# Float32r products that read their streamed operand from two halves in turn

## The chip, the cores and the metric

The kernel runs on one core of one Trainium2 chip. The metric is the device time of one execution in microseconds; lower is better. Times named before and after are medians of several executions.

## The reference

One transformer layer over 256 tokens of width 2048, in float32: a gated feed-forward, a token mixer with eight attention heads and four mLSTM heads, and a second gated feed-forward. Each is preceded by a modulation and followed by a layer norm. Almost all of the work lies in the weight matrices.

```
def _swiglu(h, w_in, w_out):                       # w_in 2048 x 11264, w_out 5632 x 2048
    gate, up = jnp.split(h @ w_in, 2, axis=-1)
    return (jax.nn.silu(gate) * up) @ w_out

def _token_mixer(h, w_in, ..., w_out):             # w_in 2048 x 6160, w_out 2048 x 2048
    z = h @ w_in
    ...                                            # attention of 8 heads, mLSTM of 4 heads
    return jnp.concatenate([y_fox, y_mlstm], axis=-1) @ w_out

def _layer(x, c, ...):
    ada = (silu(c) @ w_ada + b_ada)[:, None, :]    # w_ada 2048 x 18432
    sh1, sc1, g1, sh2, sc2, g2, sh3, sc3, g3 = jnp.split(ada, 9, axis=-1)
    h = _swiglu(_modulate(x, sh1, sc1), ffn1_w_in, ffn1_w_out)
    x = _layernorm(ALPHA * x + 0.5 * (1 + g1) * h, ln1_g, ln1_b)
    h = _token_mixer(_modulate(x, sh2, sc2), w_in, ..., w_out)
    x = _layernorm(ALPHA * x + (1 + g2) * h, ln2_g, ln2_b)
    h = _swiglu(_modulate(x, sh3, sc3), ffn2_w_in, ffn2_w_out)
    return _layernorm(ALPHA * x + 0.5 * (1 + g3) * h, ln3_g, ln3_b)
```

## The kernel before

**Split products.** A float32 operand is cut into two float32r parts: hi, a rounded copy made by ScalarE (line 155), and lo, the difference made by VectorE (line 156). A product of two float32 tiles is then the sum of three float32r products, hi by hi, hi by lo and lo by hi, added up in one PSUM tile. This is mm3 (lines 406 to 409), which all large products go through. In the profile the three show as lines 407, 408 and 409. A matmul takes a stationary operand, 128 columns that are loaded as weights before it (PEld in the profile), and a streamed one, whose words go through the array.

**Two forms.** Where features come out on partitions (the input products of the feed-forwards, tiles s, gu_f, fh, fs; the heads' inputs, tiles pr), the weight matrix is stationary and the 256 tokens are streamed, xhi or xlo, 256 columns. Where tokens come out on partitions (the output products o_f and o_mx, the mixer's tiles mo, b_mv, b_fv, and ge, gf), the tokens are stationary and 512 columns of weights are streamed; two blocks in b_mv and b_fv are 256 and 264 columns wide, since 8 gate columns follow the values there. Some early products of mo and ge take whole float32 operands (line 734), which need no split.

**Order.** The first feed-forward's input runs in four parts as the modulated features become ready (first_in, to about 308 us), then in column blocks (ffn_in, tiles gu_f, to 528 us); then its output products with three widths of columns (out_proj, to 774 us), a boundary with the layer norm, the mixer (to 1163 us), another boundary, the second feed-forward's input (tiles ge, fh, gf, fs, gu_f, to 1667 us) and its output (to 1910 us), and the last layer norm. Beside all this the weights of the modulation, w_ada, are loaded and summed on VectorE (line 170) a few rows at a time, put between the steps.

**Weights.** SyncE issues one load of 1 MB per step (line 382) into one of three raw buffers; hi and lo have six buffers each. Small gaps between tiles (gap) fix where in SBUF the tiles lie.

**PSUM.** Five tiles of 128 x 512 float32 take the large products, three more the small ones. A finished tile is read by ScalarE or VectorE: the gated product in ffn_in (lines 432, 433), the residual update in out_proj (lines 486, 488, 497, 499), copies elsewhere. In the two staged inputs (first_in, and fh with fs) the parts are kept in hT in the order in which PSUM held them, and the gated product comes later (lines 949 and 950; 1593 to 1597).

Of the kernel before, what the change touches and what calls it, by code (L numbers as in the profile page):

```python
# [14 lines left out]
P = 128  # L15
# [17 lines left out]
def layer_kernel(  # L33
# [344 lines left out]
    def load_w(src, nk, w, name, by_parts=False, behind=None, into=None):  # L378
# [5 lines left out]
        for q in range(nk // h):  # L384
# [18 lines left out]
            for kk in range(h):  # L403
                yield q * h + kk, hi[:, kk, :], lo[:, kk, :]

    def mm3(o, ah, al, bh, bl, start, stop):
        PE.matmul(o, ah, bh, start=start, stop=False)  # L407
        PE.matmul(o, ah, bl, start=False, stop=False)  # L408
        PE.matmul(o, al, bh, start=False, stop=stop)  # L409


    def cols_form_a(src, c0, outs, xT, name, npump, halves=(0, 1)):
        xhi, xlo = xT
        for kh in halves:
            for k8, hi, lo in load_w(src[kh * 1024:(kh + 1) * 1024, c0:c0 + 256], 8, 256, f"{name}_{kh}"):
                k = kh * 8 + k8
                for f in range(2):
                    fs = slice(f * P, (f + 1) * P)
                    mm3(outs[f], hi[:, fs], lo[:, fs], xhi[:, k, :], xlo[:, k, :],
                        k == 8 * halves[0], k == 8 * halves[-1] + 7)  # L420
            npump()

    def ffn_in(w, xT, hT, j0, tag, npump):
        for j in range(j0, DFF // 256):
            ps = [mm_tile(f"gu_{tag}{j}_{f}") for f in range(2)]
            for gu in range(2):
                last = gu and j == DFF // 256 - 1
                cols_form_a(w, gu * DFF + j * 256, [p[:, gu * T:(gu + 1) * T] for p in ps], xT,
                            f"{tag}i{j}_{gu}", (lambda: None) if last else npump)
            for f in range(2):  # L430
                sg = sm.tile([P, T], F32, tag="sg", bufs=2, name=f"sg_{tag}{j}_{f}")
                S.activation(sg, ps[f][:, :T], AF.Silu)
                pin["h"] = V.tensor_tensor(out=hT[:, 2 * j + f, :], in0=sg, in1=ps[f][:, T:], op=ALU.mult).ins
        for _ in range(2):
            npump()

# [2 lines left out]
    def out_proj(w, rows, nk, tag, npump, finish, before=None, turned=False, spare=None, fine=None):  # L439
# [12 lines left out]
        for width in (1024, 512, 512):  # L452
# [29 lines left out]
            def add_halves(outs, col=col):  # L482
                for c, o in enumerate(outs):
                    cs = slice(col + c * 256, col + (c + 1) * 256)
                    r = res[:, 1, cs]
                    V.tensor_tensor(out=o[:, :256], in0=o[:, :256], in1=gate[:, cs], op=ALU.mult)
                    yield
                    V.tensor_tensor(out=r, in0=r, in1=o[:, :256], op=ALU.add)
                    yield
                    add_stats(cs)  # L490
                    yield

            def add_up(a, ps=ps, col=col, bs=range(nb), stats=True):
                for b in bs:
                    cs = slice(col + b * 512, col + (b + 1) * 512)
                    r = res[:, a, cs]
                    V.tensor_tensor(out=ps[a, b], in0=ps[a, b], in1=gate[:, cs], op=ALU.mult)
                    yield
                    V.scalar_tensor_tensor(out=r, in0=r, scalar=ALPHA, in1=ps[a, b],
                                           op0=ALU.mult, op1=ALU.add)  # L500
                    yield
                    if a and stats:
                        add_stats(cs)
                    elif stats:
                        V.bn_stats(st[0][:, col // 512 + b, :], r)
                    yield
# [216 lines left out]
    def cols_1024(raws, xs, ws, split_, load, ps, xT, npump, u0, u1, ready=None):  # L723
        def split_products(a, k, hi, lo, start, stop):
            ts_ = slice(a * P, (a + 1) * P)
            for b in range(2):
                bs = slice(b * 512, (b + 1) * 512)
                mm3(ps[a, b], xT[0][:, k, ts_], xT[1][:, k, ts_], hi[:, bs], lo[:, bs], start, stop)

        for a, u in ((0, 0), (0, 1), (0, 2), (1, 2)) if raws else ():  # L730
            for q in range(2):
                k = 2 * u + q
                for b in range(2):
                    PE.matmul(ps[a, b], xs[a, k], raws[u][:, q, b * 512:(b + 1) * 512], start=k == 4 * a, stop=False)
        for w in ws:
            split_products(1, *w, False, False)
        for u in range(u0 + len(raws), u1):
            if u == u1 - 2 and ready:
                ready()
            for w in split_.get(u) or load(u):  # L740
                for a in range(2):
                    split_products(a, *w, w[0] == 2 * u0, w[0] == 2 * u1 - 1)
            npump()
# [178 lines left out]
    def first_in(j, i, ws):  # L922
        gu, q = i % 2, i // 2
        pss = [mm_tile(f"s{j}_{i}_{b}") for b in range(2)]
        def one(h, k, hi, lo, start, stop):
            for b, ps in enumerate(pss):
                fs = slice((2 * b + h) * P, (2 * b + h + 1) * P)
                mm3(ps[:, h * T:(h + 1) * T], hi[:, fs], lo[:, fs], xT[0][:, k, :], xT[1][:, k, :], start, stop)

        ws = list(ws)  # L930
        if i + j == 0:
            for w in ws:
                for h in range(2):
                    one(h, *w, w[0] + h == 0, w[0] + h == 4)
        else:
            for h in range(2):
                for w in ws:
                    one(h, *w, w[0] == 4 * j, w[0] == 4 * j + 3)
        for b, ps in enumerate(pss):
            f0 = 2 * NS * gu + 4 * q + 2 * b  # L940
            part = first_part(f0, f0 + 2).rearrange("p f t -> p (f t)")
            if j == 0:
                copied[i] = S.copy(part, ps).ins
            else:
                pin["h"] = V.tensor_tensor(out=part, in0=part, in1=ps, op=ALU.add).ins
            if j == 3 and gu:
                for f in range(f0, f0 + 2):
                    sg = sm.tile([P, T], F32, tag="sg", bufs=2, name=f"sgs{f}")
                    S.activation(sg, hT[:, f - 2 * NS, :], AF.Silu)
                    V.tensor_tensor(out=hT[:, f - 2 * NS, :], in0=sg, in1=first_part(f, f + 1)[:, 0, :], op=ALU.mult)  # L950

    ws = []

# [225 lines left out]

    def use_fv(col, a, ps, w):  # L1180
        wv = min(w, 1024 - col)
        out_ = S.copy(yF[:, col // P:(col + wv) // P, a * P:(a + 1) * P],
                      ps[:, :wv].rearrange("p (h n) -> p h n", n=P))
        if wv < w:
            out_ = S.copy(gz[:, a, 0:8], ps[:, wv:w])
            V.tensor_tensor(out=gz[:, a, 0:8], in0=gz[:, a, 0:8], in1=gbias[:, 0:8], op=ALU.add)
        return out_
# [73 lines left out]
    def use_mv(col, a, ps, w):  # L1261
        wv = min(w, 1024 - col)
        for i in range(0, wv, MV):
            out_ = S.copy(yM[(col + i) // MV][:, a, :MV], ps[:, i:i + MV])
        if wv < w:
            S.copy(gz[:, a, 12:16], ps[:, wv:wv + 4])
            out_ = S.copy(gz[:, a, 8:12], ps[:, wv + 4:w])
            V.tensor_tensor(out=gz[:, a, 8:12], in0=gz[:, a, 8:12], in1=gbias[:, 12:16], op=ALU.add)
            V.tensor_tensor(out=gz[:, a, 12:16], in0=gz[:, a, 12:16], in1=gbias[:, 8:12], op=ALU.add)
        return out_  # L1270
# [143 lines left out]

    for a in range(2):
        for h in range(NMH):
            emptied[0] = S.activation(og[h][:, a, :MV], mps[a, h // 2][:, h % 2 * MV:(h % 2 + 1) * MV],
                                      AF.Sigmoid).ins
    cols_form_b(C_FV, 512, [256, 264], use_fv, "fv")
    cols_form_b(C_MV, 512, [256, 264], use_mv, "mv")  # L1420
# [8 lines left out]
    def fox_heads(h0, name, before):  # L1429
        qs = {}  # L1430

        def queries():
            for h in range(h0, h0 + 4):
                qs[h] = new_qk(f"qs{h}", before(h))
                S.mul(qs[h][:, 0, :], psq[h - h0], QK_SCALE)

        psq = form_a_four(C_FQ + h0 * P, f"f{name}")
        psk = form_a_four(C_FK + h0 * P, f"f{name}k", queries)
        for h in range(h0, h0 + 4):
            S.copy(qs[h][:, 1, :], psk[h - h0])  # L1440
            side.append(fox_head(qs[h], h))

    for i, c0 in enumerate((C_MQ, C_MK)):
# [4 lines left out]
        for u in us:  # L1448
            V.memset(u[:, :, 0:4], 0.0)
        for h in range(NMH):  # L1450
            S.copy(us[h // 2][:, h % 2, 4:], ps[h])
        if i == 0:
            os_ = [new_qk(f"o_{h}", ()) for h in range(NMH)]
        side.append(conv_part(us, os_, i))
# [89 lines left out]

    for a in range(2):
        for g in range(2):
            S.copy(part(a, g), gups[a, g])

    def half_in(j, kh, tag):
        ps = [mm_tile(f"{tag}{j}_{f}") for f in range(2)]  # L1550
# [25 lines left out]
    cols_1024([], {}, [], {}, gu_load, gups, xT, at(R_B), 4, 8, lambda: [None for _ in mb])  # L1576
    for a in range(2):
        for g in range(2):
            V.tensor_tensor(out=part(a, g), in0=part(a, g), in1=gups[a, g], op=ALU.add)
        S.activation(part(a, 0), part(a, 0), AF.Silu)  # L1580
        V.tensor_tensor(out=part(a, 0), in0=part(a, 0), in1=part(a, 1), op=ALU.mult)
    for j in range(2, 10):
# [7 lines left out]
        for f in range(2):  # L1590
# [3 lines left out]
            V.tensor_tensor(out=u, in0=u, in1=ps[f][:, T:], op=ALU.add)  # L1594
            sg = sm.tile([P, T], F32, tag="sg", bufs=2, name=f"sgf{i}")
            S.activation(sg, g, AF.Silu)
            V.tensor_tensor(out=g, in0=sg, in1=u, op=ALU.mult)
    npool.release()
    ffn_in(W2, xT, hT, 10, "f2", at(R_B))
    need(14)  # L1600
# [44 lines left out]
```

## Time and profile before

| | |
|---|---|
| median of 3 runs | 1921.97 us (1921.58 to 1922.64) |
| span of the profiled execution | 1920.7 us |
| its chain that ended last: TensorE, VectorE, DMA | 91%, 4%, 3% |
| HBM read over the span | 506.71 MB, 265 GB/s |

No time of its own is listed for the profiled execution beside its span; the span stands 1.3 us below the median. A group row of the profile reads: line, engine, operation, written tile <- read tiles, shape, count | busy us, mean ns of one | idle time of the engine before them and who ended it. Records of successive matmuls overlap, so their mean is longer than the time between their starts. A row of the chain reads: start, duration, what. A row of the windows reads: window in us, its length, then for each engine its busy time and number of instructions, the granted clock of TensorE, the share of the DMA engines and GB/s.

### The profile page before, as it was taken

What the parts mean: (1) busy time and instruction counts of PE and PEld (TensorE: products, weight loads), DVE (VectorE), ACT (ScalarE), POOL (GpSimd) and SP (SyncE); (2) the same over time, 40 slices, a digit from 0 to 9 for tenths busy, and PEclk for the clock granted to TensorE, in tenths of its full rate; (3) what the DMA queues carried; (4) which work ended last, traced back from release to release, by engine and by line L of the source; (5) the groups of instructions that cost most, each with busy time, mean ns of one, the idle gap of its engine ahead of it and who ended that gap; (6) DMA issues with size and microseconds to landing.
All of it is one profiled execution on the core that took longest, in us unless ns stands there. A gap on an engine that the chain in (4) does not pass through costs nothing.

```text
span 1920.7 us, 32475 instructions
## 1 busy us (share of the span) xinstructions
PE 1892.3 (99%) x13161; PEld 1730.3 (90%) x13161; DVE 1482.5 (77%) x1855; ACT 948.7 (49%) x1358; POOL 60.0 (3%) x88
## 2 busy tenths in 40 slices
PE   7999999999999999999999999999999999999997
PEld 5999999999988887699999886999999999988886
DVE  6788988877788898878889888867766665555776
ACT  3554454443454555845565545555444444444562
POOL 1111100000000000100000000000000000000000
PEclk9999999999999999999999999999999999999999
DMA  9978968999898786499878983987777765655552
GB/s 365 379 279 310 314 235 273 331 311 329 282 343 304 263 308 222 147 312 323 306 270 308 310 306 130 336 293 241 257 251 260 248 212 188 241 188 187 195 196 89
DMA packets 283710, 510.92 MB, mean 266 GB/s; under 512 B 10626, under 2 KB 134178, under 8 KB 282536
## 3 DMA queue, kind: packets, MB, share of 16 engines
q1 hardware_dynamic: 276024, 482.10, 73.3%
q0 software_dynamic: 7536, 26.75, 4.2%
q8 instruction: 103, 1.69, 0.4%
q14 instruction: 47, 0.39, 0.1%
HBM read 506.71 MB, written 2.10 MB: 265 GB/s over the span
## 4 chain that ended last, share of the span: by engine, by line
PE 91%; DVE 4%; DMA 3%; ACT 1%; issue 1%; POOL 0%; SPq 0%; DVEq 0%; ACTq 0%; POOLq 0%
PE gu_f L409 8%; PE gu_f L407 8%; PE gu_f L408 8%; PE o_f L407 8%; PE o_f L409 7%; PE o_f L408 7%; PE s L409 4%; PE s L407 4%; PE s L408 4%; PE fh L407 2%; PE fh L409 2%; PE fh L408 2%; PE fs L407 1%; PE fs L408 1%; PE fs L409 1%; PE o_mx L407 1%
## 5 line engine op out<-in xcount | busy, mean ns | idle before, releaser
L170 DVE SCALAR_TENSOR_TENSOR acc<-ar,csil,acc 128x1024 f32<-128x1024 f32 (+1 forms) x167 | 211.6, 1268 | 67.2 <-DMA ar<-in_w_ada_dram 66.5
L409 PE MATMUL s<-xhi_f,lo_s 128*128 128x256 f32 x768 | 212.3, 277 | 0.7 <-DVE lo_s L156 0.6
L407 PE MATMUL s<-xhi_f,hi_s 128*128 128x256 f32 x768 | 212.6, 277 | 0.3 <-ACT xhi_f L336 0.3
L408 PE MATMUL s<-xlo_f,hi_s 128*128 128x256 f32 x768 | 212.4, 277 | 0.0
L409 PE MATMUL gu_f<-xhi_f,lo_f2i 128*128 128x256 f32 x768 | 212.0, 276 | 0.0
L407 PE MATMUL gu_f<-xhi_f,hi_f2i 128*128 128x256 f32 x768 | 212.0, 276 | 0.0
L408 PE MATMUL gu_f<-xlo_f,hi_f2i 128*128 128x256 f32 x768 | 212.0, 276 | 0.0
L156 DVE TENSOR_TENSOR lo_f2i<-raw_f2i,hi_f2i 128x1024 fp32r<-128x1024 f32 x96 | 117.6, 1225 | 94.1 <-ACT hi_f2i L155 94.1
L409 PE MATMUL gu_f<-xhi_f,lo_f1i 128*128 128x256 f32 x640 | 176.8, 276 | 0.1
L407 PE MATMUL gu_f<-xhi_f,hi_f1i 128*128 128x256 f32 x640 | 176.7, 276 | 0.0
L408 PE MATMUL gu_f<-xlo_f,hi_f1i 128*128 128x256 f32 x640 | 176.7, 276 | 0.0
L155 ACT CAST hi_f2i<-raw_f2i 128x1024 fp32r<-128x1024 f32 x96 | 100.8, 1050 | 135.4 <-PE gu_f L408 122.9
L155 ACT CAST hi_s<-raw_s 128x1024 fp32r<-128x1024 f32 x96 | 99.5, 1051 | 129.3 <-PE s L408 84.4
L409 PEld LDWEIGHTS s<-xhi_f,lo_s 128*128 128x128 f32 x768 | 144.1, 188 | 1.1 <-DVE lo_s L156 1.1
L408 PEld LDWEIGHTS s<-xlo_f,hi_s 128*128 128x128 f32 x768 | 144.2, 188 | 0.3 <-DVE xlo_f L339 0.3
L407 PEld LDWEIGHTS s<-xhi_f,hi_s 128*128 128x128 f32 x768 | 144.0, 188 | 0.4 <-ACT xhi_f L336 0.4
L407 PEld LDWEIGHTS gu_f<-xhi_f,hi_f2i 128*128 128x128 f32 x768 | 144.2, 188 | 0.2
L408 PEld LDWEIGHTS gu_f<-xlo_f,hi_f2i 128*128 128x128 f32 x768 | 144.2, 188 | 0.2
L409 PEld LDWEIGHTS gu_f<-xhi_f,lo_f2i 128*128 128x128 f32 x768 | 144.2, 188 | 0.0
L170 DVE SCALAR_TENSOR_TENSOR gate<-ar,csil,gate 128x1024 f32<-128x1024 f32 (+1 forms) x94 | 117.5, 1251 | 29.8 <-DMA ar<-in_w_ada_dram 29.4
L156 DVE TENSOR_TENSOR lo_f2o<-raw_f2o,hi_f2o 128x1024 fp32r<-128x1024 f32 x86 | 105.2, 1223 | 43.3 <-ACT hi_f2o L155 43.3
L156 DVE TENSOR_TENSOR lo_s<-raw_s,hi_s 128x1024 fp32r<-128x1024 f32 x96 | 115.3, 1220 | 25.5 <-ACT hi_s L155 25.4
(484 smaller groups left out, 5522.9 us busy)
## 6 DMA issues: line engine op xcount, KB each, us to landing
ar<-in_w_ada_dram SPq DMA_DIRECT2D x230, 512.0 KB, 5.3
raw_f2i<-in_ffn_w_in_dram SPq DMA_DIRECT2D x48, 1024.0 KB, 5.1
raw_s<-in_ffn_w_in_dram SPq DMA_DIRECT2D x47, 1024.0 KB, 7.5
raw_f1o<-in_ffn_w_out_dram SPq DMA_DIRECT2D x44, 1024.0 KB, 7.5
raw_f2o<-in_ffn_w_out_dram SPq DMA_DIRECT2D x44, 1024.0 KB, 5.1
raw_f1i<-in_ffn_w_in_dram SPq DMA_DIRECT2D x40, 1024.0 KB, 7.8
ar<-in_w_ada_dram POOLq DMA_DIRECT2D x45, 512.0 KB, 6.6
raw_mxo<-in_w_out_dram SPq DMA_DIRECT2D x16, 1024.0 KB, 7.6
```

What stands on the lines that cost most here:

```text
L155: S.copy(hi, src)
L156: return V.tensor_tensor(out=lo, in0=src, in1=hi.bitcast(F32), op=ALU.subtract)
L170: V.scalar_tensor_tensor(out=acc, in0=raw, scalar=csil[:, k:k + 1], in1=acc, op0=ALU.mult, op1=ALU.add)
L407: PE.matmul(o, ah, bh, start=start, stop=False)
L408: PE.matmul(o, ah, bl, start=False, stop=False)
L409: PE.matmul(o, al, bh, start=False, stop=stop)
```

## The change

The streamed operand of a split product is given to TensorE through woven: a view with the columns as (n, 2), in which the words of the first half and of the second alternate. The halves are 128 words long in the short form and 256 in the long one, so a word and the next lie 512 or 1024 bytes apart in SBUF. A streamed operand whose width is no multiple of 256 stays as it is. The columns of the result in PSUM are then woven too: column 2n is the n-th of the first half, 2n + 1 the n-th of the second. So whoever reads PSUM takes unwoven, two runs with a step of two words, and writes to halves, two plain runs. Where parts are only added up, they stay woven in SBUF, and the gated product unweaves them there. The stationary operands, the loads, the splits and all sizes are as before, and each engine has the same instructions in the same order.

```diff
+    def woven(b):
+        if b.shape[-1] % 256:
+            return b
+        return b.rearrange("p (a n) -> p n a", a=2)
+
+    def unwoven(ps):
+        return ps.rearrange("p (n a) -> p a n", a=2)
+
+    def halves(v):
+        return v.rearrange("p (a n) -> p a n", a=2)
+
     def mm3(o, ah, al, bh, bl, start, stop):
+        bh, bl = woven(bh), woven(bl)
         PE.matmul(o, ah, bh, start=start, stop=False)
         PE.matmul(o, ah, bl, start=False, stop=False)
         PE.matmul(o, al, bh, start=False, stop=stop)
...
                 sg = sm.tile([P, T], F32, tag="sg", bufs=2, name=f"sg_{tag}{j}_{f}")
-                S.activation(sg, ps[f][:, :T], AF.Silu)
-                pin["h"] = V.tensor_tensor(out=hT[:, 2 * j + f, :], in0=sg, in1=ps[f][:, T:], op=ALU.mult).ins
+                S.activation(halves(sg), unwoven(ps[f][:, :T]), AF.Silu)
+                pin["h"] = V.tensor_tensor(out=halves(hT[:, 2 * j + f, :]), in0=halves(sg),
+                                           in1=unwoven(ps[f][:, T:]), op=ALU.mult).ins
...
-                    r = res[:, 1, cs]
-                    V.tensor_tensor(out=o[:, :256], in0=o[:, :256], in1=gate[:, cs], op=ALU.mult)
+                    r, o = halves(res[:, 1, cs]), unwoven(o[:, :256])
+                    V.tensor_tensor(out=o, in0=o, in1=halves(gate[:, cs]), op=ALU.mult)
                     yield
-                    V.tensor_tensor(out=r, in0=r, in1=o[:, :256], op=ALU.add)
+                    V.tensor_tensor(out=r, in0=r, in1=o, op=ALU.add)
...
-                    V.tensor_tensor(out=ps[a, b], in0=ps[a, b], in1=gate[:, cs], op=ALU.mult)
+                    o = unwoven(ps[a, b])
+                    V.tensor_tensor(out=o, in0=o, in1=halves(gate[:, cs]), op=ALU.mult)
                     yield
-                    V.scalar_tensor_tensor(out=r, in0=r, scalar=ALPHA, in1=ps[a, b],
+                    V.scalar_tensor_tensor(out=halves(r), in0=halves(r), scalar=ALPHA, in1=o,
                                            op0=ALU.mult, op1=ALU.add)
...
-                    PE.matmul(ps[a, b], xs[a, k], raws[u][:, q, b * 512:(b + 1) * 512], start=k == 4 * a, stop=False)
+                    PE.matmul(ps[a, b], xs[a, k], woven(raws[u][:, q, b * 512:(b + 1) * 512]), start=k == 4 * a,
+                              stop=False)
...
-                    V.tensor_tensor(out=hT[:, f - 2 * NS, :], in0=sg, in1=first_part(f, f + 1)[:, 0, :], op=ALU.mult)
+                    V.tensor_tensor(out=halves(hT[:, f - 2 * NS, :]), in0=unwoven(sg),
+                                    in1=unwoven(first_part(f, f + 1)[:, 0, :]), op=ALU.mult)
...
-            S.copy(qs[h][:, 1, :], psk[h - h0])
+            S.copy(halves(qs[h][:, 1, :]), unwoven(psk[h - h0]))
...
-            V.tensor_tensor(out=g, in0=sg, in1=u, op=ALU.mult)
+            V.tensor_tensor(out=halves(g), in0=unwoven(sg), in1=unwoven(u), op=ALU.mult)
```

The copies out of PSUM that are left out here (the values, the gates and the heads' inputs of the mixer, the early parts of the second feed-forward) change in the same way.

More of the change, by code (lines that the diff above doesn't have):

```diff
@@ L409, in mm3, with cols_form_a @@
         PE.matmul(o, al, bh, start=False, stop=stop)
-    def cols_form_a(src, c0, outs, xT, name, npump, halves=(0, 1)):
+    def cols_form_a(src, c0, outs, xT, name, npump, khs=(0, 1)):
         xhi, xlo = xT
-        for kh in halves:
+        for kh in khs:
             for k8, hi, lo in load_w(src[kh * 1024:(kh + 1) * 1024, c0:c0 + 256], 8, 256, f"{name}_{kh}"):
@@ L419, in cols_form_a @@
                     mm3(outs[f], hi[:, fs], lo[:, fs], xhi[:, k, :], xlo[:, k, :],
-                        k == 8 * halves[0], k == 8 * halves[-1] + 7)
+                        k == 8 * khs[0], k == 8 * khs[-1] + 7)
             npump()
@@ L1181, in use_fv @@
         wv = min(w, 1024 - col)
-        out_ = S.copy(yF[:, col // P:(col + wv) // P, a * P:(a + 1) * P],
-                      ps[:, :wv].rearrange("p (h n) -> p h n", n=P))
+        src = ps[:, :wv].rearrange("p (h n) -> p h n", n=P)
+        if w == wv:
+            src = ps[:, :w].rearrange("p (m h) -> p h m", h=2)
+            if w > 2 * P:
+                src = src.rearrange("p a (h n) -> p a h n", n=P)
+        dst = yF[:, col // P:(col + wv) // P, a * P:(a + 1) * P]
+        if len(src.shape) == 4:
+            dst = dst.rearrange("p (a h) n -> p a h n", a=2)
+        out_ = S.copy(dst, src)
         if wv < w:
@@ L1263, in use_mv @@
         for i in range(0, wv, MV):
-            out_ = S.copy(yM[(col + i) // MV][:, a, :MV], ps[:, i:i + MV])
+            y, src = yM[(col + i) // MV][:, a, :MV], ps[:, i:i + MV]
+            if w == 2 * MV:
+                src = unwoven(ps)[:, i // MV, :]
+            elif w == MV:
+                y, src = halves(y), unwoven(src)
+            out_ = S.copy(y, src)
         if wv < w:
@@ L1416, in layer_kernel @@
         for h in range(NMH):
-            emptied[0] = S.activation(og[h][:, a, :MV], mps[a, h // 2][:, h % 2 * MV:(h % 2 + 1) * MV],
+            emptied[0] = S.activation(og[h][:, a, :MV], unwoven(mps[a, h // 2])[:, h % 2, :],
                                       AF.Sigmoid).ins
@@ L1434, in queries @@
                 qs[h] = new_qk(f"qs{h}", before(h))
-                S.mul(qs[h][:, 0, :], psq[h - h0], QK_SCALE)
+                S.mul(halves(qs[h][:, 0, :]), unwoven(psq[h - h0]), QK_SCALE)
         psq = form_a_four(C_FQ + h0 * P, f"f{name}")
@@ L1450, in layer_kernel @@
         for h in range(NMH):
-            S.copy(us[h // 2][:, h % 2, 4:], ps[h])
+            S.copy(halves(us[h // 2][:, h % 2, 4:]), unwoven(ps[h]))
         if i == 0:
@@ L1546, in layer_kernel @@
         for g in range(2):
-            S.copy(part(a, g), gups[a, g])
+            S.copy(halves(part(a, g)), unwoven(gups[a, g]))
     def half_in(j, kh, tag):
@@ L1578, in layer_kernel @@
         for g in range(2):
-            V.tensor_tensor(out=part(a, g), in0=part(a, g), in1=gups[a, g], op=ALU.add)
+            V.tensor_tensor(out=halves(part(a, g)), in0=halves(part(a, g)), in1=unwoven(gups[a, g]), op=ALU.add)
         S.activation(part(a, 0), part(a, 0), AF.Silu)
```

## The prediction

> **What bounds the kernel now.** I read the page from the top: busy times, slices, the chain that ended last.
>
> ```profile
> span 1920.7 us, 32475 instructions
> ...
> PE 1892.3 (99%) x13161; PEld 1730.3 (90%) x13161; DVE 1482.5 (77%) x1855; ACT 948.7 (49%) x1358; POOL 60.0 (3%) x88
> ...
> PEclk9999999999999999999999999999999999999999
> ...
> PE 91%; DVE 4%; DMA 3%; ACT 1%; issue 1%; POOL 0%; SPq 0%; DVEq 0%; ACTq 0%; POOLq 0%
> ```
>
> TensorE is busy for 99% of the span, at the full granted clock, and the chain that sets the end lies on it for 91%. So the time is close to the number of products times their pitch, the time from one product's start to the next one's. A record's own duration is longer than the pitch, because records overlap; the pitch is read by counting products in a window that holds only one kind. The first row below is such a window of the second feed-forward's input products (tile gu_f, 256 columns each, columns: window, length, busy time and count of each engine, clock, DMA share, GB/s), the second a window that holds only output products (o_f, 512 columns).
>
> ```profile
> 1500.00:1590.00 90.00, 90.00 (x796) 90.00 (x795) 3.35 (x8) 3.08 (x8) 1.00 0.68 230
> ...
> 1702.00:1800.00 98.00, 98.00 (x430) 1.00 0.57 189
> ```
>
> 90.00 us / 796 = 113.1 ns per 256-column product; 98.00 us / 430 = 227.9 ns per 512-column product. Is that as fast as the array can go? The trace holds products in plain float32 beside the float32r ones, and they answer in part. These are rows of the chain (start, duration, what), then the group row of line 734 (count | busy us, mean ns | idle before).
>
> ```profile
> 776.82 9.44 PE mo L734 x22
> ...
> 978.54 0.87 PE nps L1367 x4
> ```
>
> ```profile
> L734 PE MATMUL mo<-raw_mo,xf 128*128 128x512 f32 x32 | 14.9, 599 | 0.1
> ```
>
> Line 734 makes 16 float32 products of 512 columns here and the group has 32 records, so one product leaves two records. They follow each other every 9.44 / 22 = 429 ns; a product takes 858 ns. A float32r product of the same shape takes 227.9, which is 3.77 times less and not 4. If the float32 product makes four passes over its columns (an estimate: the rows show two records, not what is inside them), one pass is 858 / 4 = 214.5 ns. The rows of line 1367 give 0.87 / 4 = 217.5 ns for a record of 257 columns, half of it 108.7, or 108.3 ns for 256 columns. Against these the float32r products lose 227.9 - 214.5 = 13.4 ns and 113.1 - 108.3 = 4.8 ns each. The durations say where the loss arises:
>
> ```profile
> L407 PE MATMUL o_f<-hi_f2o,hh 128*128 128x512 f32 x324 | 127.3, 393 | 0.0
> L408 PE MATMUL o_f<-lo_f2o,hh 128*128 128x512 f32 x324 | 125.7, 388 | 0.0
> ...
> L409 PE MATMUL gu_f<-xhi_f,lo_f2i 128*128 128x256 f32 x768 | 212.0, 276 | 0.0
> ...
> L409 PE MATMUL b_fv<-hi_fv,xlo_mx 128*128 128x256 f32 x32 | 9.0, 283 | 0.0
> ```
>
> With the same shape a product takes 393 ns when it streams hi and 388 when it streams lo, and 276 against 283 ns when the streamed tile is another. The array does the same work in each, so part of the excess comes from reading the operands out of SBUF: the place where the change acts.
>
> **The change, part by part.**
>
> (1) No instruction is added, removed or moved on any engine; no DMA and no wait is new. What changes is the order in which 9504 products of 256 columns and 2928 of 512 columns in float32r (counted from the loops: 4224 gu, 2304 s, 1536 fh and fs, 768 pr and so on; 2064 o_f, 384 o_mx and so on) read the streamed operand: word 0 of the first half, word 0 of the second, word 1 of the first, and so on. Neighbouring words now lie 512 or 1024 bytes apart. The 192 products of 264 columns keep their order. 32 float32 products of line 734 change too; by the same estimate they take four passes where float32r takes one, so they are not pressed for words, and I cost them at nothing (32 x 858 ns = 27 us if they doubled, a small part of the upper bound below).
>
> One nanosecond of pitch is worth 9504 ns = 9.5 us in the short form and 2.9 us in the long. No product in the trace streams an operand with a step, so the price is bounded from both sides. Below: the excess goes wholly, 4.8 x 9504 = 45.6 us and 13.4 x 2928 = 39.2 us, together -84.8 us. Above: each word costs a second array step, and the products slow to the pace of a float32 record, 113.1 to 217.5 and 227.9 to 429: 104.4 x 9504 = 992 us and 201.1 x 2928 = 589 us, together +1581 us. The rows that stand nearest are the first kind: the pitch now is within 6% of the lower bound and 90% away from the upper, and the excess is shown to hang on where operands lie. I take two thirds of the lower bound, because only part of the excess is seen to move with the operands: 30.4 + 26.1 = -56.5 us, which is a pitch of 109.9 ns and 219.0 ns.
>
> [...]
>
> (2) PSUM is read back with a step of two words by ScalarE and VectorE. Within a stage this is hidden:
>
> ```profile
> L432 ACT ACTIVATE sg_f<-gu_f 128x256 f32<-128x256 f32 x44 | 16.9, 384 | 21.8 <-PE gu_f L409 21.7
> ...
> L433 DVE TENSOR_TENSOR hT2b<-sg_f,gu_f 128x256 f32<-128x256 f32 x20 | 8.4, 418 | 6.0 <-ACT sg_f L432 6.0
> ```
>
> A pair of gu tiles is read by two of each of these, 1.6 us one after the other, while TensorE works 192 x 113.1 ns = 21.7 us on the next pair in other PSUM tiles. It is on the chain only where a stage ends:
>
> ```profile
> 763.39 0.71 DVE o_f L497
> ...
> 764.12 0.70 DVE res L499
> ...
> 1910.05 0.44 DVE o_f2last L486
> ...
> 1910.51 0.43 DVE res L488
> ```
>
> The first two stand again at the second boundary (1163.79 and 1164.53 us). No row of the trace has a stepped read of PSUM. From nothing to a doubling that is 0 to 2 x 1.41 + 0.87 = 3.7 us. A gain from a step has no reason here. The nearest rows are a pass with PSUM and one without:
>
> ```profile
> L156 DVE TENSOR_TENSOR hl<-hT2a,hh 128x512 fp32r<-128x512 f32 x35 | 23.8, 687 | 13.9 <-ACT hh L155 13.9
> ...
> L499 DVE SCALAR_TENSOR_TENSOR res<-res,o_f 128x512 f32<-128x512 f32 x16 | 10.7, 681 | 0.1
> ```
>
> 681 ns with PSUM as one input against 687 from SBUF alone: the memory does not set VectorE's pace now, so I take 0.
>
> (3) The stepped reads from SBUF in the gated products of the staged parts (lines 950 and 1597) are on VectorE off the chain; it has time, by the rows that follow.
>
> (4) What is late next, when TensorE goes 3% faster? Rows of 100 us windows (PE, PEld, DVE, ACT, POOL busy, clock, DMA share, GB/s):
>
> ```profile
> 0.00:100.00 100.00, 88.37 (x641) 76.50 (x641) 72.05 (x98) 46.56 (x64) 14.54 (x27) 1.00 0.99 364
> 100.00:200.00 100.00, 100.00 (x883) 100.00 (x883) 88.59 (x104) 46.36 (x58) 17.00 (x24) 1.00 0.85 302
> ...
> 400.00:500.00 100.00, 100.00 (x878) 99.74 (x877) 75.51 (x78) 41.85 (x49) 1.07 (x2) 1.00 0.95 312
> ```
>
> VectorE would go from 89% to 91% at 100 to 200 us, and the loads at 400 to 500 us from 312 to 321 GB/s, while the first window moves 364. Neither is full. If both stages kept their present pace, 3% of 400 us, 12 us, of the gain would go; I take 0 and keep 12 us for the range.
>
> **Sum.** -56.5 + 0 + 0. The profiled execution spans 1920.7 us; the median of the runs is 1921.97, 1.3 us more, which I take as what lies around the span. 1921.97 - 56.5 = 1865 us.
>
> **The rivals.**
>
> *Half the word rate (slower).* If a word from another place costs a second array step, the pitch becomes that of the float32 records, and the time 1922 + 1581 = 3503 us. It decides as soon as a product takes over 113.1 ns. For it speaks that no product in the trace has ever read this way, and that float32r asks for words at four times the pace of float32, so a slower read shows at once; against it, that the excess over the quarter of a float32 product is now only 6%, so the read is not far from keeping up.
> [...]
>
> *Milder (slower).* The weight load of the next product reads SBUF meanwhile; if a streamed operand that moves between two places meets it twice as often, the excess doubles: +84.8 us, 2007 us.
>
> *The weight loads bound the short form (faster, by less).* Every product loads its own weights:
>
> ```profile
> L408 PEld LDWEIGHTS gu_f<-xlo_f,hi_f2i 128*128 128x128 f32 x265 | 49.7, 188 | 0.0
> ...
> L408 PEld LDWEIGHTS o_f<-lo_f2o,hh 128*128 128x128 f32 x143 | 26.8, 188 | 5.9
> ```
>
> In the window of gu_f the loads are busy without a pause (90.00 of 90.00 us), in that of o_f they idle. If loads cannot follow closer than 113 ns, only the long form gains: 1922 - 26 = 1896 us. Against it: loads of 188 ns every 113 ns overlap already, and the 256-column products of b_fv have the same loads and yet differ.
>
> *No change.* The order of reads doesn't matter, since what is lost is lost at the start of a product or in the weight load: 1922 to 1926 us with part (2). A read that the hardware turns back into a contiguous one, so that the change does nothing, ends here too; the words' step is in the instruction, so I see no ground for that.
>
> **How the numbers follow.** The forecast, the excess goes in good part, 0.60; weight loads bound the short form 0.13; no change 0.08; milder slowing 0.06; half rate 0.13. The likeliest gives 1865 us. Its own range runs from all of the excess gone (1837, less 6 us for the rounding of the 0.87 us row: 1831) to a third of it with 12 us given back (1906). Leaving out the two slower cases, 0.19, the range reaches from 1831 over 1896 to no change with both small costs, 1930 us. A measurement of this kernel tells about 0.2% (4 us) from no change. Faster by more: 0.60 + 0.13 = 0.73; within: 0.08; slower by more: 0.06 + 0.13 = 0.19.
>
> **What would show it.** Right: a window of gu_f alone holds 90 us / 109.9 ns = 819 products and one of o_f 98 us / 219.0 ns = 447; the mean durations 393 and 388 come together; the passes at 763.39 and 764.12 keep 0.71 and 0.70 us. Weight loads as the bound: gu_f stays at 796 and o_f rises. Half rate: gu_f falls to some 414. Wrong in part (4): idle time of TensorE behind lo or raw tiles between 100 and 500 us. Wrong in part (2): rows of line 499 well above 681 ns. The forecast fails if the excess is not made by the order of reads at all.

## The result, and the profile after

| | before | after |
|---|---|---|
| median of the runs | 1921.78 us (1920.61 to 1922.64, 4 runs) | 1891.51 us (1889.97 to 1899.08, 4 runs) |
| span of the profiled execution | 1920.7 us | 1889.9 us |

The ratio is 0.9847, with an interval of 0.9828 to 0.9866: 30 us faster. The forecast was 56.5 us and 1865 us; its range held the time.

First the windows of the changed kernel (columns as before): the same two stretches that the prediction counted, then the whole output of the first feed-forward with the start of the boundary behind it, and that of the second without its last tile.

```profile
1500.00:1590.00 90.00, 90.00 (x804) 89.83 (x804) 55.59 (x56) 38.85 (x46) 0.00 (x0) 1.00 0.67 222
...
1702.00:1800.00 98.00, 98.00 (x456) 85.82 (x455) 69.90 (x78) 53.27 (x64) 0.00 (x0) 1.00 0.61 204
...
522.30:766.70 244.40, 234.70 (x1075) 202.68 (x1073) 216.67 (x258) 127.16 (x169) 2.08 (x2) 0.99 0.81 284
1650.80:1868.30 217.50, 217.50 (x1010) 190.48 (x1009) 155.81 (x173) 120.56 (x150) 0.00 (x0) 1.00 0.60 201
```

And the same two stages in the kernel before:

```profile
528.50:775.50 247.00, 246.24 (x1075) 200.43 (x1073) 216.66 (x257) 129.80 (x169) 2.08 (x2) 1.00 0.80 279
1667.50:1898.30 230.80, 230.80 (x1010) 189.06 (x1009) 156.54 (x173) 120.71 (x150) 0.00 (x0) 1.00 0.56 189
```

gu_f goes from 113.1 to 90.00 / 804 = 111.9 ns, o_f from 227.9 to 98.00 / 456 = 214.9 ns. (A count takes in the records that the ends of the window cut, so it is off by up to 1 ns: from start to start the same stretches have 113.3 and 111.7 ns, and 228.9 and 215.8.) In the second output TensorE never idles in either kernel, and its 1010 products take 13.3 us less. The first output has 1075 products, but in the changed kernel it holds 244.40 - 234.70 = 9.7 us without TensorE, against 0.8 before, and is only 2.6 us shorter. The same gain in pitch was kept in one place and lost in the other.

Now the groups by shape of the changed kernel, against the 393 and 388 ns and the 276 and 283 ns that the prediction started from:

```profile
L419 PE MATMUL o_f<-hi_f2o,hh 128*128 128x512 f32 x324 | 122.8, 379 | 0.0
L420 PE MATMUL o_f<-lo_f2o,hh 128*128 128x512 f32 x324 | 122.8, 379 | 0.0
...
L421 PE MATMUL gu_f<-xhi_f,lo_f2i 128*128 128x256 f32 x768 | 211.2, 275 | 0.0
...
L421 PE MATMUL b_fv<-hi_fv,xlo_mx 128*128 128x256 f32 x32 | 8.8, 275 | 0.0
```

The durations of one shape have come together, whatever tile is streamed. The rows of PSUM readback on the chain, at the second boundary and at the end:

```profile
1152.53 0.71 DVE o_mx L511
...
1153.26 0.70 DVE res L513
...
1879.29 0.44 DVE o_f2last L499
...
1879.76 0.43 DVE res L501
```

0.71, 0.70, 0.44 and 0.43 us, as before: the step of two words in PSUM costs VectorE nothing here. Over the whole kernel VectorE is busy for 1482.5 us before and 1482.1 after, ScalarE for 948.7 and 947.6. A row of the chain that did get longer is that of the whole float32 products (line 734 before, 748 now):

```profile
1166.16 11.89 PE ge L748 x22
```

11.89 / 22 = 540 ns where the record took 9.44 / 22 = 429. (The chain of this execution is followed back only to 1007 us, so its shares by engine can't be set beside the 91% of before.)

Where TensorE waits is told by the view of waits (who, for whom: us in total, times, longest), first of the kernel before, then of the changed one:

```profile
ACT hi_f1o L155 <- DMA raw_f1o<-in_ffn_w_out_dram: 23.1, 11, 4.8
```

```profile
ACT hi_f1o L155 <- DMA raw_f1o<-in_ffn_w_out_dram: 73.5, 24, 6.8
...
PE o_f L420 <- DVE lo_f1o L156: 3.4, 2, 1.8
PE bc L183 <- ACT ahi L155: 2.8, 1, 2.8
...
PE o_f L419 <- DVE res L513: 2.3, 1, 2.3
PE pr_fb L421 <- DVE lo_fb L156: 2.2, 1, 2.2
PE o_mx L421 <- DVE ylo L156: 2.1, 1, 2.1
```

In the first output ScalarE, which makes hi, now stands 73.5 us behind the loads of w_out instead of 23.1, and TensorE has to pause. The loads in that stage ran at 279 GB/s before and at 284 now.

**The sum, from the starts of the products in the two traces** (means without pauses, over the whole kernel): the long form fell from 229.6 to 216.2 ns, 13.4 x 2928 = -39.2 us; the short form from 113.7 to 111.65 ns, 2.05 x 9504 = -19.5 us; 64 float32 records at 111 ns more, +7.1 us; pauses of TensorE, from 19 to 39 us, +20. Together -31.6 us; the spans differ by 30.8. More than half of the pauses' 20 us fell in the first output: at 13.4 ns its 1056 long products should have given 14 us, and the stage gave 2.6. The next largest part fell at the end of the mixer: the last 240 products of o_mx should have given 3 us and took 1.3 us longer.

### The profile page after: what moved, and what is told of

Its sections match the earlier page's. It is cut to its first block, busy times and chain, and to the rows that moved or that the text cites. A ratio compares the mean times of both kernels' runs of the same rounds, so it can differ in the third digit from the quotient of the medians.

```text
span 1889.9 us, 32481 instructions
## 1 busy us (share of the span) xinstructions
PE 1847.1 (98%) x13161; PEld 1718.6 (91%) x13161; DVE 1482.1 (78%) x1855; ACT 947.6 (50%) x1358; POOL 60.0 (3%) x88
## 3 DMA queue, kind: packets, MB, share of 16 engines
HBM read 506.71 MB, written 2.10 MB: 269 GB/s over the span
## 5 line engine op out<-in xcount | busy, mean ns | idle before, releaser
L170 DVE SCALAR_TENSOR_TENSOR acc<-ar,csil,acc 128x1024 f32<-128x1024 f32 (+1 forms) x167 | 211.7, 1269 | 65.6 <-DMA ar<-in_w_ada_dram 64.7
L170 DVE SCALAR_TENSOR_TENSOR gate<-ar,csil,gate 128x1024 f32<-128x1024 f32 (+1 forms) x94 | 117.6, 1252 | 27.2 <-DMA ar<-in_w_ada_dram 26.7
L155 ACT CAST hi_f1o<-raw_f1o 128x1024 fp32r<-128x1024 f32 x86 | 89.4, 1044 | 88.0 <-DMA raw_f1o<-in_ffn_w_out_dram 73.5
```

The lines of the kernel that those rows point to most:

```text
L155: S.copy(hi, src)
L170: V.scalar_tensor_tensor(out=acc, in0=raw, scalar=csil[:, k:k + 1], in1=acc, op0=ALU.mult, op1=ALU.add)
```

## The experiments

Theory A, after the result: the woven order brings every product to the pace of the array or of its weight load; the float32 products lose; and the rest of the gain is taken back by loads that are now late, in the first output above all. The rivals are named in each expectation.

### The pitch by itself

A kernel that leaves the layer out and runs series of 48 products, back to back, each series with another order, place or width of the streamed operand.

```python
    def weave(v, a=2):
        return v.rearrange("p (a n) -> p n a", a=a)
    ...
        for i in range(count):
            PE.matmul(out(ps[:m, :n]), w[:, i % 8, :m], view(src[:, i // 2 % 4, :]), start=i == 0, stop=i == count - 1)
```

> Leaves the whole layer out: series of 48 products each (24 in float32) that differ in the streamed view, its place and the number of stationary columns; the pitch of each series is what counts, not the time. Theory A (the excess is a collision between the streamed reads and the reads of the weight load, the weave ends it, and what is left in the short form is the pace of the weight loads): 512 columns plain 224 to 237 ns, differing between the four places a to d; plain with 64 stationary columns clearly nearer to 216; woven 215 to 216 at all four places; 256 columns woven 111 to 112 with 128 stationary columns and 109 to 110 with 64; 272 and 320 columns woven 116 and 136. Theory B (in the short form a part of the read excess is left, the loads bound nothing): 256 columns woven 111 to 112 with 64 stationary columns too, 272 and 320 columns woven 118 to 119 and 138 to 139. Float32 records of 512 columns: 429 plain, 540 woven, as in the trace of the changed kernel; with plain reads and a stepped output 429 if the step in PSUM costs nothing.

Groups of this kernel; busy time of 48 records is about 47 pitches and one duration, so 11.0 us is 226 ns and 10.5 us 215:

```profile
L66 PE MATMUL plain_woven<-plain,wts 128*128 128x512 f32 x48 | 26.1, 703 | 0.0
L66 PE MATMUL long_evens<-mov,wts 128*128 128x512 f32 x48 | 21.8, 632 | 0.0
L66 PE MATMUL plain_out<-plain,wts 128*128 128x512 f32 x48 | 20.8, 592 | 0.0
L66 PE MATMUL plain_flat<-plain,wts 128*128 128x512 f32 x48 | 20.8, 592 | 0.0
L66 PE MATMUL long_quarters<-mov,wts 128*128 128x512 f32 x48 | 13.8, 451 | 0.0
L66 PE MATMUL long_flat_d<-mov,wts 128*128 128x512 f32 x48 | 11.4, 394 | 0.0
...
L66 PE MATMUL long_flat_a<-mov,wts 128*128 128x512 f32 x48 | 11.0, 389 | 0.0
...
L66 PE MATMUL long_woven_d<-mov,wts 128*128 128x512 f32 x48 | 10.5, 379 | 0.0
L66 PE MATMUL long_woven_a<-mov,wts 128*128 128x512 f32 x48 | 10.5, 379 | 0.0
...
L66 PE MATMUL short_flat_a<-mov,wts 128*128 128x256 f32 x48 | 5.9, 283 | 0.0
...
L66 PE MATMUL mid_woven_x<-mov,wts 128*128 128x272 f32 x48 | 5.7, 279 | 0.0
...
L66 PE MATMUL short_woven_a<-mov,wts 128*128 128x256 f32 x48 | 5.5, 275 | 0.0
L66 PE MATMUL short_woven_m<-mov,wts 128*64 128x256 f32 x48 | 5.4, 272 | 0.0
```

From start to start: a plain read of 512 words takes 226.7, 229.2, 232.5 or 233.3 ns as the operand begins 0, 64, 128 or 192 bytes further on; woven it is 215.8 at all four places, and 216.3 with the halves 1056 bytes apart. Words taken from four quarters in turn: 283 ns. All even words and then all odd ones: 451. In the short form plain reads take 114.0 to 119.9, woven ones 111.6 to 111.7, and with 64 stationary columns in place of 128, 109.1. Woven products of 272 and 320 columns take 115.9 and 135.8. So the short form stops at its weight load: with half of the weights (loads of 136 ns in place of 192), or with more columns to stream, the woven product keeps one pace, 0.42 ns a column: 106.7 ns for the 256 columns between 109.1 and 215.8, 19.9 ns for the 48 between 115.9 and 135.8. A plain read of 512 columns does not reach it, from 226.7 ns up.

Theory A missed one point: with 64 stationary columns a plain read of 512 words still takes 230.3 ns, so in the long form it does not lose its time to the weight load. In the short form the smaller load does help the plain read, from 119.9 to 113.9 ns, which is still 4.8 above the woven one: there a part of the loss hangs on the load, and the series do not show how.

### One width at a time

The kernel after, with only the products of 512 columns woven, and with only those of 256.

```diff
+    WOVEN = (512,)
+
     def woven(b):
-        if b.shape[-1] % 256:
+        if b.shape[-1] not in WOVEN:
             return b
```

> Only operands of 512 columns are woven, those of 256 are read plainly. Theory A: o_f2 and the other long products go to 216 ns, 2928 x 12 ns = 35 us are saved, 7 us are given back by the float32 products of line 748 (64 records x 111 ns) and some 12 to 15 us in the part that reads ffn1_w_out, which becomes bound by its loads: 1907 to 1911 us. Rival (the loss in that part comes from the faster part before it, so that loads fall behind there): the part keeps its gain when the short form is slow, 1892 to 1896 us.

> Only operands of 256 columns are woven, those of 512 (float32 products of the early parts among them) are read plainly. Theory A: 9504 x 2.0 ns = 19 us saved, pitch of gu_f 111.7 ns, line 748 at 429 ns again: 1902 to 1904 us. Rival (the stepped reads of PSUM and of SBUF cost the other engines what the products gain): 1910 us and more.

Long only: 1907.11 us, ratio 0.9939 (0.9916 to 0.9962), as theory A has it. Short only, WOVEN = (256,): 1907.18 us, ratio 0.9942 (0.9921 to 0.9963), 3 us above theory A's 1902 to 1904 and 3 below the rival's 1910. Windows of gu_f and of o_f of the long one, then gu_f of the short one:

```profile
1500.00:1590.00 90.00, 90.00 (x795) 89.91 (x794) 53.64 (x52) 37.88 (x43) 0.00 (x0) 1.00 0.68 222
1720.00:1818.00 98.00, 98.00 (x456) 85.82 (x455) 70.82 (x79) 53.42 (x65) 0.00 (x0) 1.00 0.61 204
```

```profile
1500.00:1590.00 90.00, 90.00 (x805) 89.84 (x804) 55.95 (x56) 38.50 (x45) 0.00 (x0) 1.00 0.69 227
```

Each width gains by itself: 456 long products in 98 us without any change to the short ones (795 in 90 us, as before), and 805 short ones without the long. Each kernel gains 11 to 12 us by its ratio, and 14 by the medians. The profiled span of the long one is 16.8 us shorter than that of before (1903.9 and 1920.7 us). That is close to 39.2 of pitch, less 7.1 of float32 and less what the pauses at long products grew by, from 4.6 to 20.1 us: 16.6. So the long form brings most of the waits, with or without the short one.

### The float32 products read plainly

The products of line 748 read their operand as it lies and write PSUM with a step of two words, so all that follows stays as in the kernel after.

```diff
-                    PE.matmul(ps[a, b], xs[a, k], woven(raws[u][:, q, b * 512:(b + 1) * 512]), start=k == 4 * a,
-                              stop=False)
+                    PE.matmul(unwoven(ps[a, b]), xs[a, k], halves(raws[u][:, q, b * 512:(b + 1) * 512]),
+                              start=k == 4 * a, stop=False)
```

> The changed kernel, but the 32 float32 products of line 748 read their streamed operand plainly, half after half, and write PSUM with a step of two words, which gives the same columns. Theory A (the 540 ns come from the woven read): 429 ns per record, 64 x 111 ns = 7 us less, 1884 to 1885 us. Rival (a stepped write to PSUM costs as much or more): records of 540 ns or above, 1891 us or more.

> The changed kernel once more, for the comparison with the next one on one chip: 1890 to 1892 us.

> The changed kernel with plain reads and a stepped output in the early float32 products, more often measured. Theory A: 6 to 7 us less than the changed kernel beside it, 1883 to 1886 us. Rival (the time that the early products win is lost again to the loads that follow): less than 3 us.

A row of the chain in the first of these runs:

```profile
1165.16 9.44 PE ge L748 x22
```

429 ns again: writing PSUM with a step costs TensorE nothing in these float32 products (429.2 ns with the step, 429.1 without, in the series); a float32r product was not tried.

The time was 1885.96 us (two values, near 1882.7 and 1889.2), ratio 0.9821 (0.98 to 0.9842). The repetition beside the kernel after itself gave 1892.3 against 1892.56 (ratios 0.9863 and 0.9861), which by the number is the rival's case, under 3 us. The 7 us are gained at TensorE, and whether the kernel keeps them is not settled: the runs of both scatter by 8 to 11 us. The two profiled executions (1894.89 us, and 1890.29 of the kernel after) show where they differ. From the first float32 product of mo to the first product of b_fv 50.6 us passed against 53.3 in the kernel after, and from the first one of ge to the second feed-forward's gu_f 223.9 against 227.3. So both stretches that hold these products kept most of the gain. The first output, which lies ahead of all of them, took 248.8 us against 245.7, so its loss can't come from them. The mixer between them took 348.3 against 341.9; whether that follows from the float32 products ahead of it is not shown.

### Half of the modulation's loads

Every second load of w_ada beside the main work is left out (the sums take the rows loaded before them), in the kernel before and in the kernel after.

```diff
         for k in range(KD):
-            raw = ap.tile(list(acc.shape), F32, tag="araw", bufs=2, name=f"ar{tag}_{k}")
-            SP.dma_start(raw, src[k * P:(k + 1) * P])
+            if k % 2 == 0:
+                raw = ap.tile(list(acc.shape), F32, tag="araw", bufs=2, name=f"ar{tag}_{k}")
+                SP.dma_start(raw, src[k * P:(k + 1) * P])
```

> The kernel before, but of the rows of w_ada that are summed in the background only every second is loaded and used twice, so half of these loads are left out; VectorE does as much as ever. Theory A (before the change TensorE hides nearly all loads): 3 to 8 us less than before, 1913 to 1919 us. Rival C (loads have nothing to do with the lost gain): the same difference as between the changed kernel and its own half-loaded form.

> The changed kernel with the same half of the background loads left out. Theory A (the gain of the long form in the part that reads ffn1_w_out, some 12 us, and some in the mixer, was lost to waits for loads): 15 to 22 us less than the changed kernel, 1870 to 1877 us; the part from the first o_f product to the boundary falls from 222 us by 10 or more, and long stalls of o_f go. Rival C (the waits come from VectorE or ScalarE, which read PSUM with a step now): at most 6 us less, 1885 us or more, and the stalls of o_f stay.

Before: 1915.61 us, ratio 0.9979 (0.997 to 0.9989), 3.1 us less than its own before. After: 1874.06 us, ratio 0.9767 (0.9748 to 0.9786), 18.5 us less than the kernel after, measured beside it (1892.56). The same loads that cost the kernel before 3 us cost the changed one 18. The window of its first output and the wait there:

```profile
523.80:761.50 237.70, 233.91 (x1075) 203.61 (x1073) 216.21 (x257) 129.01 (x169) 2.08 (x2) 0.99 0.71 242
```

```profile
ACT hi_f1o L155 <- DMA raw_f1o<-in_ffn_w_out_dram: 26.5, 12, 3.7
```

TensorE idles 237.70 - 233.91 = 3.8 us instead of 9.7, the stage is 6.7 us shorter, where theory A had said 10 or more, and ScalarE's wait is back from 73.5 to 26.5 us. The larger part comes back in the mixer, here from the first product of b_fv to the end of o_mx. These are its windows in the kernels before, after, before with half of the loads, and after with half:

```profile
827.30:1174.80 347.50, 343.59 (x2308) 314.38 (x2306) 290.15 (x430) 187.30 (x337) 6.98 (x7) 1.00 0.85 294
```

```profile
820.20:1163.50 343.30, 335.31 (x2308) 313.33 (x2306) 291.16 (x433) 186.54 (x337) 6.99 (x7) 0.99 0.87 299
```

```profile
826.30:1167.40 341.10, 341.10 (x2307) 312.96 (x2307) 291.12 (x432) 188.60 (x337) 6.01 (x7) 1.00 0.71 240
```

```profile
814.40:1145.20 330.80, 330.02 (x2308) 310.97 (x2307) 292.26 (x436) 187.50 (x337) 6.02 (x7) 1.00 0.73 248
```

The mixer of the changed kernel gets 12.5 us shorter without half of the loads, that of the kernel before 6.4, by one trace each. So loads cost time in the mixer already before the change, and about twice as much after it. In the first output they cost the kernel before next to nothing: it has only 0.8 us of idle time there to lose.

A second path is not ruled out. VectorE, which makes lo, waits for the rows of w_ada itself: at line 170 for 91 us over the whole kernel after (64.7 for acc, 26.7 for gate), and for 18 with half of the loads. In the first output that wait is 10.8 us beside ScalarE's 73.5, so there the late loads of w_out are the likelier cause. In the mixer it is 32 us beside some 52 of ScalarE behind its loads of w_in and w_out, and the runs do not tell the two apart.

Is it their bytes, or their places in SyncE's queue, where a load that waits for its buffer holds back the load of a weight matrix behind it? In the kernel after, SyncE's queue waits 183.2 us, in 124 waits, at the loads of w_ada (line 189) until VectorE is done with acc (line 170). In the next kernel all of these loads stay, in their order, but bring half of the columns.

```diff
+            if k < 2:
+                raws[k] = ap.tile(list(acc.shape), F32, tag="araw", bufs=2, name=f"ar{tag}_{k}")
+            raw, w = raws[k % 2], acc.shape[-1] // (1 if k < 2 else 2)
+            SP.dma_start(raw[..., :w], src[k * P:(k + 1) * P, ..., :w])
```

> The kernel after with every load of ada_rows kept in number and order, but each after the second of a block brings only half of its columns (about 54 MB less in all); the sums over old columns are wrong, their work is the same. Theory A (the waits come from the bytes that the modulation's loads move beside the weight loads): most of the 18 us that half the loads gave comes back, 1873-1879 us, and the wait of hi_f1o for its loads falls from 73 us to 20-40. Rival Q (they come from the places that these loads take in SyncE's queue, where a load that waits for its buffer holds back the weight load behind it): the queue is as long as before, so 1886-1895 us and the wait of hi_f1o stays over 60 us.

> The kernel after with every second load of ada_rows left out, as once before (1874.06 us), here beside half_width on the same chip: 1871-1878 us by either theory. Theory A: within 4 us of half_width. Rival Q: 12-20 us below it.

1879.07 us, ratio 0.9787 (0.9766 to 0.9808), beside 1873.28 us and 0.9754 (0.9736 to 0.9771). The wait in the kernel of half the width:

```profile
ACT hi_f1o L155 <- DMA raw_f1o<-in_ffn_w_out_dram: 22.8, 12, 3.5
```

The queue kept its length, and the wait fell all the same: mainly it is the bytes. By the ratios half the width gives 0.0074 of the 0.0107 that half of the loads give (from 0.9861 of the kernel after). Theory A was 0.1 us outside its range and said 4 us between the two where 5.8 were measured. The kernels differ in bytes too (HBM reads of 455.33 and 447.99 MB, against 506.71 in the kernel after), which would be some 2 us at 18.5 us for 58.7 MB; the rest may be the queue's, or scatter, since the two intervals overlap.

### Why a plain read loses

Left open by the first series: why is a plain read slow, and an interleaved one fast? A second kernel without the layer, with other runs, steps and widths.

> Leaves the whole layer out: series of 48 products (24 in float32) that differ in the order of the streamed words. [...] Rival (a collision with the weight loads): plain with 32 stationary columns near 218.

Groups of this kernel:

```profile
L62 PE MATMUL step_four<-mov,wts 128*128 128x512 f32 x48 | 22.3, 639 | 0.0
...
L62 PE MATMUL step_two<-mov,wts 128*128 128x512 f32 x48 | 21.8, 629 | 0.0
L62 PE MATMUL step_three<-mov,wts 128*128 128x512 f32 x48 | 21.8, 628 | 0.0
...
L62 PE MATMUL halves_by_two<-mov,wts 128*128 128x512 f32 x48 | 16.5, 513 | 0.0
...
L62 PE MATMUL flat_m_third<-mov,wts 128*32 128x512 f32 x48 | 11.3, 394 | 0.0
L62 PE MATMUL flat<-mov,wts 128*128 128x512 f32 x48 | 11.0, 389 | 0.0
...
L62 PE MATMUL halves_by_one<-mov,wts 128*128 128x512 f32 x48 | 10.5, 379 | 0.0
```

Start to start: halves in turn by one word 215.8 ns, by two words 339.8, by four 250.3, by sixteen 240.1; steps of two, three and four words 451, 450 and 460; 32 stationary columns, plain, 231.6. Of 256 columns, a step of four takes 233.3 ns and a step of eight 217.9; of 384, plain takes 174.4 and halves in turn 162.4. The rival falls: it had 218 ns for 32 stationary columns. Nor does the time grow with the step: two, three and four cost nearly the same, and of 256 columns a step of eight takes less than one of four. What stays is the facts: steps of two, three, four and eight cost 0.85 to 0.91 ns a word, about twice the 0.42 of the halves in turn, and of the orders tried only two halves word by word reach 215.8 ns. The mechanism is open.

## Why the prediction was right, and where it was wrong

**Part (1), the sign: right.** The excess was made by the order of reads: the same words in another order take 215.8 ns and not 226.7 to 233.3. The two rivals that slow the kernel fell, the half rate and the milder one; the doubt was well founded, since a step of two words does run at 451 ns. That float32r asks for words at four times the pace of float32 was an estimate: the kernel before shows 3.77 times (858 and 227.9 ns for 512 columns). Nor is a read slow by the distance to its next word alone: two words off it takes 451 ns, 1024 bytes off 215.8. Why just this order is fast the prediction did not derive, and no run explains it.

**Part (1), the sizes: right only in their sum, by luck.** The prediction took two thirds of each excess. The long form lost all of it, 39.2 us where 26.1 were taken. That this is the lower bound to the tenth is chance: the bound was reckoned from 227.9 to 214.5 ns, and the pitch went from 229.6 to 216.2 over the whole kernel. The quarter of a float32 product, 214.5, was 1.3 ns under the best pace of the series; that such a product makes four passes was the author's estimate, near the measured 3.77, and no run shows it. The short form lost 19.5 where 30.4 were taken: it goes down to 111.65 ns and not to 109.9, because there the weight load is the bound (109.1 with half of it). So the rival "weight loads bound the short form" was half true: a bound, but at 111.6 ns and not at 113.1. The argument against it, that loads of 188 ns overlap already, said nothing of how close they can follow. Together -58.7 us against -56.5: one part was too small by 13.1 us and the other too large by 10.9.

**Part (1), the float32 products: wrong.** They were costed at nothing, "not pressed for words". They lost: 429 to 540 ns a record, 7.1 us. The upper bound of 27 us held; the reason did not. The 192 products of 264 columns, which keep their plain read, lost a little too: hi by hi from 123.3 to 133.5 ns and hi by lo from 121.2 to 125.5, together 0.9 us. They do so where the 256-column products beside them are woven (hi by hi 133.7 ns in the kernel with only those woven) and not where only the long ones are (122.2).

**Part (2): right.** The passes kept their 0.71 and 0.70 us.

**Part (4): the step that failed.** It took 0 and kept 12 us for the range, for "neither is full". The first output, where the gain per product is the largest, was not among its windows: it read 100 to 200 and 400 to 500 us. That stage already had ScalarE behind its loads for 23.1 us, at 279 GB/s, and a mean under the highest window says nothing of how much more a stage can get while the w_ada loads go beside. Pauses took 20 us; with half of the w_ada loads gone, 18.5 us come back, of which the kernel before would have had 3.1. By the traces 6.7 of them lie in the first output and 12.5 in the mixer, which is not among its windows either. With part (1) near its size, this and the float32 products are what separates 1865 from 1891.5.

**What would show it.** 819 and 447 products in the two windows were named, 804 and 456 came; the durations of hi and lo came together, as named. Idle time behind lo tiles came too, but between 600 and 712 us and in the mixer at 949 us, and not at 100 to 500. The range's upper end of 1930 us is not worked out in the prediction: no change with part (2) alone gives 1926.

## What to carry to other kernels

Where float32r products follow each other at more than the woven series did (215.8 ns for 512 columns, 111.6 for 256), try the streamed operand as two halves in turn, word by word, measured in a series of its own first; keep float32 products out of it (540 ns against 429 here), and never take a step (451 to 460 ns) or longer runs (240.1 to 339.8) for the same thing. Then look stage by stage for the one whose loads already make the engine ahead of TensorE wait: a faster TensorE gains there only what the loads allow (2.6 of 14 us in the first output here), and other loads beside them are the place to look for the rest.

## What the runs showed that was not expected

A step of two in the streamed operand halves the pace in float32r (451 ns for 512 words against 227) and costs 5% in a float32 record (452 against 429), while two interleaved halves gain 5 to 7.5% over a plain read in float32r (215.8 against 226.7 to 233.3) and lose 26% in float32 (540 against 429).

After some pauses of a little over 2 us TensorE ran at half pace. The view of waits of the changed kernel, above, has one of 2.1 us at tile o_mx; these are windows right after it:

```profile
1115.60:1119.00 3.40, 3.40 (x10) 2.68 (x9) 3.34 (x3) 0.00 (x0) 0.00 (x0) 0.51 0.96 330
1119.20:1122.00 2.80, 2.80 (x15) 2.44 (x14) 2.41 (x4) 1.60 (x2) 0.00 (x0) 1.00 0.76 242
```

The granted clock was 0.51 for 3.4 us, with eight products 427 to 430 ns apart, and 1.00 after. So the pause cost some 1.7 us more than its own length (8 x 212 ns). The changed kernel has two more such stretches, from 743.4 and 951.6 us, behind pauses of 2.8 and 2.2 us; the kernel before has one, from 970.4 us, behind a pause of 2.3. So some 3 of the 20 us that the pauses grew by are half pace, reckoned in the same way. Not every such pause did that: after the one of 2.3 us at 640 us the products kept 216 ns, and the repetition of the kernel after has one of 3.0 us at 641 us without a half-pace stretch behind it.
